# Spreading the norm's factors by two transfers, and building attention's bias rows on GpSimd

## The chip, the cores and the metric

The kernel runs on one core of one Trainium2 chip. The metric is the device time of one execution in microseconds; the median of three runs of the kernel before is 1729.15 us (1728.78 to 1729.55). One further execution was recorded by the hardware profiler, and all rows below come from it. Engines carry the profile's names: PE is the matrix engine (PEld its weight loads), DVE the vector engine, ACT the scalar engine, POOL is GpSimd, SP only issues transfers. SPq, ACTq and POOLq mark transfers that SP, ACT and POOL issue.

## The reference

A two-layer encoder trunk on 256 tokens of width 1024, in float32. Each layer is a token mixer and then an expert retrieval (PEER), with an RMS norm ahead of each of these four stages:

```python
def _rmsnorm(x, g):
    y = xf * lax.rsqrt(jnp.mean(xf * xf, axis=-1, keepdims=True) + RMS_EPS)
    return (y * g)

# layer 0: gated short convolution     layer 1: windowed attention, +-128 tokens
x = x + mixer(_rmsnorm(x, g_mixer))
x = x + _peer(_rmsnorm(x, g_ffn), w_q, subkeys, u, v)

# attention's bias: one row of 16 head values per bucket of the distance key - query
bias = rel_bias[_t5_bucket(rel)]        # rel_bias is 32 x 16
logits = where(abs(rel) <= 128, scores + bias, -1e30)
```

`_t5_bucket` gives each distance 0 to 7 a bucket of its own and then ever longer runs of distances one bucket, 16 buckets for each sign. In PEER each token finds 128 of 16384 experts by product keys; the kernel multiplies all rows of the two expert tables u and v with all tokens and weighs the unwanted ones with zero.

## The kernel before, in words

**Stages.** Convolution mixer (about the first 98 us of the profile), PEER of layer 0 (to about 868 us), attention (to about 952 us), PEER of layer 1, final norm. In each, every weight tile (128x1024, float32) is loaded by SP as `raw`, rounded to `hi` by ACT (L196), and the rest `lo` = raw - hi is formed by DVE (L197); PE then multiplies hi and lo with the two parts of the activations. `hi` has three buffers and `lo` two (in places four), so the tiles run about two ahead of PE.

**The norm's factors.** `turned_x` transposes the residual for a stage without the norm's factor; the factor, one number per token, is found meanwhile on DVE (`scale`, L419 to L428) and stands in two columns of `stat`, tokens on partitions. Later steps need it along the free dimension, the same 256 numbers on all 128 partitions: the tile `yb`. `factors` (L569) makes it: two transposes on PE of the broadcast column into a bank `pyb` of PSUM, and one copy by ACT (L574).

**Who reads `yb`.** In the convolution `mixed` (L619, L626); in PEER `normed` (L965), a background step; in attention L893 (`yq`), L895 (the two key tiles) and L896 (the first query tile). The first scores of attention (`psc`, tile 0) need L895 and L896. In PEER `yb` is later used again as `far`, which holds places and gates of the indirect additions.

**Attention's bias rows.** `load_buckets` (L744) loads, in the convolution stage, a 33x511 table of ones and zeros (which bucket, or outside the window) three times and the 32x16 values; `bias_rows` (L754) splits the values in three bfloat16 parts on DVE; `product` multiplies them by one matmul (`pbias`), DVE negates and reverses the result (L766), and POOL writes the 16x511 rows to `bias_dram`, from where they are read in PEER of layer 0.

**What sets the order.** Each engine runs its own instructions in program order as a scheduler laid them down, from the order of the code and its own estimates; `issue_after` pins one instruction behind another. POOL's queue holds, ahead of the indirect additions of a PEER stage (L706): the clearing of `table` in 1 MB pieces (L694, sixteen of them, each behind the one before), the load of the subkeys (L932), and whatever else is issued by GpSimd. Transfers issued by POOL share one queue.

Of the kernel before, what the change touches and what calls it, by code (L numbers as in the profile page):

```python
# [8 lines left out]
F32 = mybir.dt.float32  # L9
# [8 lines left out]
P = 128  # L18
# [58 lines left out]
def trunk_kernel(  # L77
# [37 lines left out]
    def transpose(*a):  # L115
        newest[:] = [PE.transpose(*a).ins]  # L116
        return newest[0]
# [15 lines left out]
    def bank(tag, name):  # L133
        if tag == "acc":
            return four_banks(False).tile([P, 512], F32, tag=tag, name=name, bufs=4)
        return ps.tile([P, 512], F32, tag=tag, name=name, bufs=2)
# [97 lines left out]
    def take(n=2):  # L234

        prefetch(n)
        return ahead.popleft()
# [76 lines left out]
    def wide_pair(b, act, between=None, last=False):  # L314

        pair = [[a.rearrange("p (k c) -> p k c", k=KC) for a in take(2 - i)] for i in range(2)]

        banks = b if isinstance(b, list) else [b[:, i] for i in range(2)]

        def one(i, k, low):  # L320
            with after_chain():
                chain[:] = [
                    matmul(banks[i][:, :T], pair[i][1][:, k], act[:, k, :T], start=False, stop=(k == KC - 1))
                    if low else matmul(banks[i], pair[i][0][:, k], act[:, k], start=(k == 0), stop=False)
                ]

        def part(i, low):
            for k in range(KC):
                one(i, k, low)

        part(0, False)
        if last:
            bg.pump()
            part(0, True)
            prefetch(1)
            for k in range(KC):
                one(1, k, False)
                one(1, k, True)
            prefetch(2)
            return bg.pump()  # L340
        if between:
            with in_turn():
                between()
        if roomy:
            prefetch(1)
            bg.pump()
        part(1, False)
        if roomy:
            prefetch(2)
        else:  # L350
            bg.pump()
        part(0, True)
        prefetch(1)
        part(1, True)
        prefetch(2)
        bg.pump()
# [209 lines left out]
            evicted[:] = [scaled]  # L566
        return xn

    def factors():  # L569

        b = bank("g", "pyb")
        for t in range(NT):
            transpose(b[:, P * t : P * t + P], stat[:, 8 + t : 9 + t].to_broadcast([P, P]), ident)
        S.copy(yb, b[:, :T])  # L574

    class Scratch:
        def __init__(self, tag, name, kb=64):
# [20 lines left out]
    def conv_mixer(sc):  # L598
        cw = sc(KC, 3)
        xn = turned_x(0, big.tile([P, KC, 2 * T], F32R, tag="xa", name="xn"))  # L600
        wait_for(nc.gpsimd.dma_start(cw, conv_w).ins, [bg.rounded])
        loaded = load_buckets(sc)
        z = big.tile([P, KC, 2 * T], F32R, tag="HB", name="z")
        ring = [(sc(2, T), sc(T + 2), sc(T)) for _ in range(2)]
        yb2 = sc(T)
        for _, ch, _ in ring:
            V.memset(ch, 0.0)

        def mixed(j, b0, b1):
            cs, ch, y = ring[j % 2]  # L610
            if j:
                sum_of_parts(cs, b0)
                V.tensor_tensor(ch[:, 1 : T + 1], cs[:, 0], cs[:, 1], ALU.mult)
                V.tensor_tensor(ch[:, 1 : T + 1], ch[:, 1 : T + 1], yb2, ALU.mult)
                gate = cs[:, 0]
                S.copy(gate, b1[:, T:])
                V.tensor_tensor(gate, b1[:, :T], gate, ALU.add)
            else:
                V.tensor_tensor(yb2, yb, yb, ALU.mult)  # L619
                V.tensor_tensor(ch[:, 1 : T + 1], b0[0][:, :T], yb2, ALU.mult)  # L620
                V.tensor_tensor(ch[:, 1 : T + 1], b0[1][:, :T], ch[:, 1 : T + 1], ALU.mult)
                gate = b1[:, :T]
            S.activation(y, ch[:, 0:T], AF.Copy, scale=cw[:, j, 0:1])
            V.scalar_tensor_tensor(y, ch[:, 1 : T + 1], cw[:, j, 1:2], y, op0=ALU.mult, op1=ALU.add)
            V.scalar_tensor_tensor(y, ch[:, 2 : T + 2], cw[:, j, 2:3], y, op0=ALU.mult, op1=ALU.add)
            V.tensor_tensor(y, y, yb, ALU.mult)  # L626
            V.tensor_tensor(y, gate, y, ALU.mult)
            S.copy(z[:, j, :T], y)
            V.tensor_tensor(z[:, j, T:], y, z[:, j, :T].bitcast(F32), ALU.subtract)

        for j in range(KC):
            roomy[:] = [True] if 0 < j < KC - 1 else []
            if j == 2:
                blank_table()
            if j == 4:
                bias_product = bias_rows(*loaded)
            if j in (2, 4, 6):
                blank_part(nc.gpsimd, bg.behind)
            b0 = two_banks("pconv") if 0 < j < KC - 1 else [bank("u", "pconv") for _ in range(2)]
            if j:  # L640
                wide_pair(b0, xn, (lambda: (factors(), mixed(*left))) if j == 1 else None)
            b1 = bank("g", "pgate")
            if j:
                wide_line(b1, xn)
            else:
                first_three([b[:, :T] for b in (*b0, b1)], xn)
            if j == 0:
                left = j, b0, b1
            else:
                mixed(j, b0, b1)  # L650
        acc = accumulators("pout")
        for k in range(KC - 2):
            rows_product(acc, take(), z[:, k, :T], z[:, k, T:], k == 0, bias_product if k == 1 else None)
            if k in (0, 3):
                blank_part(nc.gpsimd, bg.behind)
        return last_rows(acc, [(take(KC - k), z[:, k, :T], z[:, k, T:]) for k in (KC - 2, KC - 1)])
# [12 lines left out]
    def wait_for(ins, others):  # L669
        for o in others:  # L670
            tc.add_manual_dep(
                ins, o.name, mybir.DependencyInfo(mybir.DependencyClass.Sync, mybir.DependencyReason.DATA),
                reason="transfers of one table in turn",
            )
# [67 lines left out]
    bias_dram = dram.tile([HEADS, 511], F32, name="bias_dram")  # L742

    def load_buckets(sc):  # L744
        oh, ohb = sc(511)[:97], sc(256).bitcast(BF16)[:97, :511]
        rb, row = sc(HEADS)[:32], sc(511)[:HEADS]
        thirds, second = sc(HEADS // 2).bitcast(BF16), sc(HEADS // 2).bitcast(BF16)[:32]
        V.memset(thirds[96:97], NEG)
        for to, t in [(rb, relb)] + [(oh[i : i + 32], buckets[0:32]) for i in (0, 32, 64)] + [(oh[96:97], buckets[32:33])]:
            wait_for(nc.gpsimd.dma_start(to, t).ins, [bg.rounded])  # L750
        return oh, ohb, rb, thirds, second, row

    def bias_rows(oh, ohb, rb, thirds, second, row):
        with tc.issue_after(bg.behind):  # L754
            V.tensor_copy(ohb, oh)
            V.tensor_copy(thirds[0:32], rb)
            V.tensor_tensor(rb, rb, thirds[0:32], ALU.subtract)
            V.tensor_copy(second, rb)
            V.tensor_copy(thirds[32:64], rb)
            V.tensor_tensor(thirds[64:96], rb, second, ALU.subtract)  # L760

        def product():
            b = bank("g", "pbias")
            with in_turn():
                matmul(b[:HEADS, :511], thirds[:97], ohb, start=True, stop=True)
            V.tensor_scalar(row, b[:HEADS, 510::-1], -1.0, None, op0=ALU.mult)  # L766
            nc.gpsimd.dma_start(bias_dram, row)

        return product

    def load_bias(sc, part):

# [14 lines left out]
    def attention(sc, last):  # L787
# [3 lines left out]
        both = big.tile([P, 2, KC, 2 * T], F32R, tag="HB", name="xo")  # L791
        bk = [bank("u", "pk")[:, :T] for _ in range(2)]
        xn, o = turned_x(2, both[:, 0], last, bk), both[:, 1]


        ring = [(sc(2, 2, T + 1), sc(2, 2, 2, P), sc(2, 2, 2)) for i in range(3)]
# [89 lines left out]
            cols_product(b0[:, :T], take(), xn)  # L886
        pair = [bank("acc", f"pv{t}") for t in range(NT)]
        all_values(0, pair)
        with in_turn():
            factors()  # L890
        with tc.issue_after(evicted[0]):
            copied[:] = [S.activation(stat[:, 10:11], eps, AF.Exp).ins]
        V.tensor_scalar(yq, yb, -1.0 / 8.0, None, op0=ALU.mult)  # L893
# [33 lines left out]
    def peer(layer, last, meanwhile):  # L927
# [247 lines left out]
        for c in range(0, NSUB, 2):  # L1175
            q = qT[(c // 4) % 2][:, c % 4 : c % 4 + 2]
            b = two_banks("pq") if c else bq
            if c == 2:
                roomy[:] = [True]
            if c in (2, 6, 10):  # L1180
                blank_part(nc.gpsimd, bg.behind)
            if c:
                wide_pair(b, xr)
            else:
                bg.pump()
                prefetch(1)
                bg.pump()
            if c:
                sum_of_parts(q, b)
            else:  # L1190
                for i in range(2):
                    S.copy(q[:, i], b[i])
            if c == 2:
                factors()
            if c >= 4 and c % 4 == 0:
                compared(c - 4)
        bg.plan(bg.cost(), 2)
# [388 lines left out]
```

## Time and profile before

| what | value |
|---|---|
| median of three runs | 1729.15 us |
| the profiled execution | 1729.1 us, span 1727.3 us (1.8 us outside the span) |
| PE busy | 1719.7 us |
| PEld busy | 1478.1 us |
| DVE, ACT, POOL busy | 1385.1, 955.2, 960.9 us |
| clock granted to PE | 0.999 |
| instructions | 28115 |

A row of the timeline reads: start, duration, engine, line of the kernel, operation, tiles written <- tiles read, shapes, count; in brackets the idle time of that engine just before and what ended it. Matmuls overlap one another, so what one costs PE is read from the distance of starts, not from its duration. A row of waits reads: who waited <- for whom: us in total, times, longest. A row of transfers reads: tiles, issuing queue, operation, count, size of one, median us from issue to landing.

### The profile page before, as it was taken

To read this page: it belongs to the slowest core of one execution; us is meant where nothing else is said; L and a number is where in the kernel's file an instruction comes from. 1 tells how busy PE (TensorE), PEld (TensorE's weight loads), DVE (VectorE), ACT (ScalarE), POOL (GpSimd) and SP (SyncE) were. 2 spreads that over 40 slices of the span, in tenths; PEclk is the share of its full clock that TensorE was granted. 3 is DMA by queue.
4 is the path that set the end of the run, shared out by engine and by line. 5 is a ranking of instruction groups with operands and counts; after the bars stand their busy time and mean duration, and the time that the engine had idled before them with its cause. 6 is when DMAs were issued, how large, how long until landed. Compare 5 with 4: busy or idle time off the path is not lost.

```text
span 1727.3 us, 28115 instructions
## 1 busy us (share of the span) xinstructions
PE 1719.7 (100%) x9659; PEld 1478.1 (86%) x9659; DVE 1385.1 (80%) x2994; ACT 955.2 (55%) x1283; POOL 960.9 (56%) x594
## 2 busy tenths in 40 slices
PE   9999999999999999999999999999999999999998
PEld 8888888888888888888898988888888888888887
DVE  8879989888777677777686899898887867777776
ACT  6556665565555444444476666655655544444444
POOL 1002888888888888000000048888888888870000
PEclk9999999999999999999999999999999999999999
DMA  7786997777779999988765779977776899998884
GB/s 261 254 284 212 287 272 193 177 181 185 180 185 237 224 236 242 293 278 261 232 206 181 261 212 288 254 193 174 182 184 169 210 232 228 238 249 262 257 260 139
DMA packets 292383, 390.92 MB, mean 226 GB/s; under 512 B 120192, under 2 KB 209824, under 8 KB 291984
## 3 DMA queue, kind: packets, MB, share of 16 engines
q1 hardware_dynamic: 86688, 314.35, 53.5%
q0 software_dynamic: 80144, 22.83, 15.2%
q10 hardware_dynamic: 125408, 51.96, 11.5%
q8 instruction: 75, 1.23, 0.3%
q14 instruction: 68, 0.56, 0.1%
HBM read 353.08 MB, written 35.95 MB: 225 GB/s over the span
## 4 chain that ended last, share of the span: by engine, by line
PE 100%; DVE 0%; ACT 0%; issue 0%; ACTq 0%
PE ph L112 41%; PE pv L112 41%; PE pq L112 7%; PE pconv L112 3%; PE psc L112 1%; PE pwo L112 1%; PE pgate L112 1%; PE pout L112 1%; PE pg L112 1%; PE ptr L116 0%; PE ppt L116 0%; PE po L112 0%; PE pk L112 0%; PE pwarm L112 0%; PE pend L112 0%; PE pyb L116 0%
## 5 line engine op out<-in xcount | busy, mean ns | idle before, releaser
L197 DVE TENSOR_TENSOR lo<-raw,hi 128x1024 fp32r<-128x1024 f32 x592 | 717.8, 1221 | 197.6 <-ACT hi L196 136.5
L196 ACT CAST hi<-raw 128x1024 fp32r<-128x1024 f32 (+1 forms) x594 | 620.8, 1047 | 437.4 <-PE pv L112 180.5
L706 POOL DMA_INDIRECT table<-route x256 | 445.3, 1740 | 133.5 <-issue 74.7
L112 PE MATMUL pv<-hi,xn 128*128 128x512 f32 (+1 forms) x2048 | 507.8, 389 | 0.0
L112 PE MATMUL ph<-xn,hi 128*128 128x512 f32 x2048 | 491.2, 391 | 0.0
L112 PEld LDWEIGHTS pv<-hi,xn 128*128 128x128 f32 x2048 | 384.3, 188 | 79.5
L112 PEld LDWEIGHTS ph<-xn,hi 128*128 128x128 f32 x2048 | 376.3, 188 | 72.8
L706 POOL DMA_INDIRECT far_table<-yb x192 | 350.9, 1828 | 58.5 <-issue 53.4
L112 PE MATMUL pv<-lo,xn 128*128 128x512 f32 x1024 | 276.9, 390 | 0.0
L112 PEld LDWEIGHTS ph<-xn,lo 128*128 128x128 f32 x2048 | 262.6, 191 | 8.7
L112 PE MATMUL ph<-xn,lo 128*128 128x256 f32 x2048 | 269.7, 283 | 0.0
L112 PEld LDWEIGHTS pv<-lo,xn 128*128 128x128 f32 x1024 | 191.5, 188 | 39.4 <-DVE lo L197 0.3
L1321 POOL DMA_DIRECT2D far_gates<-far_table x44 | 23.8, 540 | 261.1 <-DMA gates<-table 108.5
L694 POOL DMA_DIRECT2D table<-blank x16 | 18.8, 1174 | 204.8 <-DVE lo L197 176.2
L706 POOL DMA_INDIRECT set_table<-yb x64 | 113.8, 1779 | 21.4 <-issue 21.4
L1383 ACT CAST xn<-hm 128x512 fp32r<-128x512 f32 x64 | 39.7, 623 | 68.5 <-PE pv L112 66.9
L364 ACT COPY hm<-ph 128x512 f32<-128x512 f32 x64 | 37.6, 587 | 65.4 <-PE ph L112 65.3
L1384 DVE TENSOR_TENSOR xn<-hm,xn 128x512 fp32r<-128x512 f32 x64 | 44.0, 690 | 34.8 <-ACT xn L1383 34.8
L1383 ACT CAST xn<-route 128x512 fp32r<-128x512 f32 x64 | 39.8, 622 | 50.0 <-PE pv L112 46.5
L1384 DVE TENSOR_TENSOR xn<-route,xn 128x512 fp32r<-128x512 f32 x64 | 44.1, 688 | 26.0 <-ACT xn L1383 26.0
L112 PE MATMUL pq<-xr,hi 128*128 128x512 f32 (+1 forms) x288 | 64.4, 370 | 0.0
L1361 ACT ACTIVATE hm<-hm 128x512 f32<-128x512 f32 x64 | 40.3, 630 | 35.8 <-DVE hm L365 35.6
(235 smaller groups left out, 1523.6 us busy)
## 6 DMA issues: line engine op xcount, KB each, us to landing
raw<-in_u SPq DMA_DIRECT2D x256, 512.0 KB, 4.6
raw<-in_v SPq DMA_DIRECT2D x256, 512.0 KB, 4.5
table<-blank POOLq DMA_DIRECT2D x16, 1024.0 KB
raw<-in_w_q SPq DMA_DIRECT2D x32, 512.0 KB, 3.7
gates<-table ACTq DMA_DIRECT2D x128, 128.0 KB, 3.9
raw<-in_w_in SPq DMA_DIRECT2D x23, 512.0 KB, 4.5
far_table<-blank ACTq DMA_DIRECT2D x10, 1024.0 KB, 8.1
far_gates<-far_table ACTq DMA_DIRECT2D x156, 64.0 KB, 4.3
```

The lines of the kernel that those rows point to most:

```text
L112: newest[:] = [PE.matmul(*a, **k).ins]
L196: bg.rounded = S.copy(hi[:, c], raw[:, c]).ins
L197: bg.behind = V.tensor_tensor(lo, raw, hi.bitcast(F32), ALU.subtract).ins
L364: S.copy(dst, b[:, :, T:])
L694: ins = queue.dma_start(dst, blank[:, None, :].to_broadcast([P, dst.shape[1], P])).ins
L706: nc.gpsimd.indirect_dma_start(to, bass.IndirectOffsetOnAxis(ap=places[:, c : c + 1], axis=0), gates[:, c : c + 1], None, compute_op=ALU.a ...
L1321: ins = (nc.gpsimd if i == 2 else nc.scalar).dma_start(f[:, i], part.rearrange("p (a e t) -> p a e t", a=2, e=2)).ins
L1361: S.activation(hm[:, j : j + 2], hm[:, j : j + 2], AF.Gelu)
L1383: copied[:] = [S.copy(a[:, 0], src).ins]
L1384: return V.tensor_tensor(a[:, 1], src, a[:, 0].bitcast(F32), ALU.subtract).ins
```

## The change

- `factors` no longer uses PE, PSUM and ACT. POOL issues a transfer of the two columns of `stat` to a scratch tensor in DRAM (`of_tokens`, 2x128, single elements of 4 bytes), and a second that reads the 256 numbers back to all 128 partitions of `yb`. The second waits for the landing of the first.
- It is called in the code right behind `turned_x` in the convolution, in attention, and in place c = 0 of the query loop of PEER (before: between the first two matmul groups of j = 1; between the two halves of the values; in place c = 2).
- `load_buckets` loads only the 32x16 values, turned to heads on partitions by 4-byte elements. `bias_rows` runs on POOL: one fill of the row with the outside value, and 31 copies of one value to a run of equal columns, negated. The 33x511 table is not loaded, and the splitting on DVE, the matmul and its eviction are gone.

```diff
-    def factors():
-        b = bank("g", "pyb")
-        for t in range(NT):
-            transpose(b[:, P * t : P * t + P], stat[:, 8 + t : 9 + t].to_broadcast([P, P]), ident)
-        S.copy(yb, b[:, :T])
+    def factors(n):
+        of_tokens = dram.tile([NT, P], F32, name=f"of_tokens{n}")
+        nc.gpsimd.dma_start(of_tokens.rearrange("t (p o) -> p t o", o=1), stat[:, 8 : 8 + NT, None])
+        nc.gpsimd.dma_start(yb, bass.AP(tensor=of_tokens.tensor, offset=of_tokens.offset, ap=[[0, P], [1, T]]))
@@ conv_mixer
         loaded = load_buckets(sc)
+        factors(0)
...
-            if j == 4:
-                bias_product = bias_rows(*loaded)
...
-                wide_pair(b0, xn, (lambda: (factors(), mixed(*left))) if j == 1 else None)
+                wide_pair(b0, xn, (lambda: mixed(*left)) if j == 1 else None)
...
-            rows_product(acc, take(), z[:, k, :T], z[:, k, T:], k == 0, bias_product if k == 1 else None)
+            rows_product(acc, take(), z[:, k, :T], z[:, k, T:], k == 0)
+            if k == 2:
+                bias_rows(*loaded)
@@ the bias rows
     def load_buckets(sc):
+        by_head, row = sc(32)[:HEADS], sc(511)[:HEADS]
+        turned = bass.AP(tensor=relb.tensor, offset=relb.offset, ap=[[1, HEADS], [HEADS, 32], [1, 1]])
+        wait_for(nc.gpsimd.dma_start(by_head[:, :, None], turned).ins, [bg.rounded])
+        return by_head, row
+
+    def bias_rows(by_head, row):
+        edges = [0, 1, 2, 3, 4, 5, 6, 7, 8, 12, 16, 23, 32, 46, 64, 91, 129]
+        wait_for(G.memset(row, -NEG).ins, [bg.behind])
+        for b, (near, beyond) in enumerate(zip(edges, edges[1:])):
+            runs = [(b, slice(255 + near, 255 + beyond))]
+            if b:
+                runs.append((16 + b, slice(256 - beyond, 256 - near)))
+            for at, c in runs:
+                G.tensor_scalar(
+                    row[:, c], by_head[:, at : at + 1].to_broadcast([HEADS, beyond - near]), -1.0, None, op0=ALU.mult
+                )
+        nc.gpsimd.dma_start(bias_dram, row)
@@ attention
         xn, o = turned_x(2, both[:, 0], last, bk), both[:, 1]
+        factors(2)
...
         all_values(0, pair)
-        with in_turn():
-            factors()
@@ peer
             else:
+                factors(1 + 2 * layer)
                 bg.pump()
...
-            if c == 2:
-                factors()
```

On POOL, in the convolution stage, the instructions move as follows (`mix_115` is the stage's scratch tile; rows with - are the order before, with + the order now):

```order
-L601 DMA mix_115<-in_conv_w 128x24
-L750 DMA mix_115<-in_relb 32x16
-L750 DMA mix_115<-in_buckets 32x511 x3
-L750 DMA mix_115<-in_buckets 1x7x73
+L600 DMA mix_115<-in_conv_w 128x24
+L747 DMA mix_115<-in_relb 16x32x1
+L572 DMA of_tokens_202<-stat 128x2x1
+L573 DMA yb<-of_tokens_202 128x256
 L694 DMA table<-blank 128x16x128 x4
```

The two transfers of the factors stand ahead of the first clearing of the table, and the loads of the bucket table are gone.

Further down the same queue, behind the fourth clearing of the table, the bias rows are built:

```order
+L753 MEMSET mix_115 16x511
+L759 TENSOR_SCALAR mix_115<-mix_115 16x1 x15
+L759 TENSOR_SCALAR mix_115<-mix_115 16x4 x4
+L759 TENSOR_SCALAR mix_115<-mix_115 16x7 x2
+L759 TENSOR_SCALAR mix_115<-mix_115 16x9 x2
+L759 TENSOR_SCALAR mix_115<-mix_115 16x14 x2
+L759 TENSOR_SCALAR mix_115<-mix_115 16x18 x2
+L759 TENSOR_SCALAR mix_115<-mix_115 16x27 x2
+L759 TENSOR_SCALAR mix_115<-mix_115 16x38 x2
+L762 DMA bias_dram<-mix_115 16x511
```

These 32 instructions and the write of the rows come ahead of one more clearing of the table and of the load of the subkeys.

On DVE, at the start of attention, the order before is (L893 to L896 read `yb`, L812 evicts the second query tile):

```order
L428 SCALAR_TENSOR_TENSOR stat<-stat 128x2
L197 TENSOR_TENSOR lo<-raw,hi 128x1024
L893 TENSOR_SCALAR mix_7315<-yb 128x256
L895 TENSOR_TENSOR mix_7315<-pk,yb 128x256 x2
L896 TENSOR_TENSOR mix_7315<-pq,mix_7315 128x256
L197 TENSOR_TENSOR lo<-raw,hi 128x1024 x2
L812 TENSOR_TENSOR mix_7315<-pq,mix_7315 128x256
```

and now (L885, L887, L888 and L806 are the same statements in the changed file):

```order
L428 SCALAR_TENSOR_TENSOR stat<-stat 128x2
L197 TENSOR_TENSOR lo<-raw,hi 128x1024 x2
L885 TENSOR_SCALAR mix_7331<-yb 128x256
L887 TENSOR_TENSOR mix_7331<-pk,yb 128x256 x2
L888 TENSOR_TENSOR mix_7331<-pq,mix_7331 128x256
L197 TENSOR_TENSOR lo<-raw,hi 128x1024
L806 TENSOR_TENSOR mix_7331<-pq,mix_7331 128x256
```

One weight tile's `lo` has moved ahead of the readers of `yb`; one stays behind them.

More of the change, by code (lines that the diff above doesn't have):

```diff
@@ L744, in load_buckets @@
     def load_buckets(sc):
[L745 to L763, printed above, removed]
-            with in_turn():
[L765 to L769, printed above, removed]
+        by_head, row = sc(32)[:HEADS], sc(511)[:HEADS]
[14 more added lines that the diff above has]
+        nc.gpsimd.dma_start(bias_dram, row)
     def load_bias(sc, part):
@@ L888, in attention @@
         all_values(0, pair)
-        with in_turn():
-            factors()
         with tc.issue_after(evicted[0]):
```

## The prediction

> **What bounds the kernel now.** I read the page first, then the waits of PE, then the timeline of PE and DVE around the five places that the change touches, and last the transfers.
>
> ```profile
> span 1727.3 us, 28115 instructions
> PE 1719.7 (100%) x9659; PEld 1478.1 (86%) x9659; DVE 1385.1 (80%) x2994; ACT 955.2 (55%) x1283; POOL 960.9 (56%) x594
> ...
> PE 100%; DVE 0%; ACT 0%; issue 0%; ACTq 0%
> ```
>
> ```profile
> PE pwarm L112 <- DVE blank L171: 1.1, 1, 1.1
> ```
>
> The first fence is the page: its span, its busy times, and the chain of work that ended last. PE is busy 1719.7 of 1727.3 us and the whole chain is PE. The second is the complete answer on what PE waited for: one wait, 1.1 us, at the start. So PE's own instructions, one after another, are the time. What leaves PE's queue is saved in full, wherever it stands; what leaves DVE, ACT or the transfers is worth nothing by itself; and any wait that the change puts in front of a matmul is paid in full. The sum has two sides: matmul time removed, and waits made.
>
> **What is removed from PE.** Four pairs of transposes (`pyb`) and the product `pbias`. Each is priced by the starts of the instructions around it against the same row without it.
>
> ```profile
> 17.06 2.00 PE L112 MATMUL pconv<-xn,hi 128*128 128x512 f32 x8
> 18.90 0.38 PE L116 MATMUL pyb<-ident,stat 128*128 128x128 f32 x2
> ...
> 20.95 2.08 PE L112 MATMUL pconv<-xn,lo 128*128 128x256 f32 x16
> ...
> 25.66 3.82 PE L112 MATMUL pconv<-xn,hi 128*128 128x512 f32 x16
> 29.31 2.08 PE L112 MATMUL pconv<-xn,lo 128*128 128x256 f32 x16
> ...
> 33.06 1.11 PE L112 MATMUL pgate<-xn,lo 128*128 128x256 f32 x8
> ```
>
> ```profile
> 105.80 3.82 PE L112 MATMUL pq<-xr,hi 128*128 128x512 f32 x16
> 109.46 2.07 PE L112 MATMUL pq<-xr,lo 128*128 128x256 f32 x16
> 111.37 0.38 PE L116 MATMUL pyb<-ident,stat 128*128 128x128 f32 x2
> ...
> 115.26 2.08 PE L112 MATMUL pq<-xr,lo 128*128 128x256 f32 x16
> 117.18 1.06 PE L112 MATMUL psc<-route 128*128 128x128 f32 x8
> ```
>
> ```profile
> 880.14 0.28 PE L112 MATMUL pv<-lo,xo 128*128 128x256 f32 x1
> ...
> 880.50 0.28 PE L112 MATMUL pv<-lo,xo 128*128 128x256 f32 x1
> ...
> 881.43 0.28 PE L112 MATMUL pv<-lo,xo 128*128 128x256 f32 x1
> ...
> 886.91 1.13 PE L112 MATMUL psc<-mix 64*128 64x256 f32 x8
> ```
>
> ```profile
> 76.75 1.98 PE L112 MATMUL pout<-hi,z 128*128 128x512 f32 x8
> 78.56 1.07 PE L112 MATMUL pout<-lo,z 128*128 128x512 f32 x4
> 79.47 1.07 PE L112 MATMUL pout<-hi,z 128*128 128x512 f32 x4
> ...
> 81.81 1.08 PE L112 MATMUL pout<-lo,z 128*128 128x512 f32 x4
> ```
>
> - Convolution: sixteen wide matmuls with the pair among them took 17.06 to 20.95, 3.89 us; the sixteen without it 25.66 to 29.31, 3.65. The pair costs 0.24.
> - PEER of layer 0: sixteen narrow ones, the pair and sixteen wide ones took 109.46 to 115.26, 5.80; alone they take 3.66 (105.80 to 109.46) and 1.92 (115.26 to 117.18), together 5.58. The pair costs 0.22. Layer 1 runs the same rows and is taken at the same 0.22.
> - Attention: a group of three matmuls takes 0.36 (880.14 to 880.50); the next two groups with the pair between them took 0.93 instead of 0.72. The pair costs 0.21.
> - `pbias`: eight wide matmuls take 1.81 (76.75 to 78.56); the eight with the product among them took 79.47 to 81.81, 2.34. It costs 0.53, more than two transposes.
>
> Sum: 0.24 + 2 x 0.22 + 0.21 + 0.53 = 1.42 us. That is 0.08% of the time. A difference under 0.2% (3.46 us) is about what a measurement of this kernel cannot tell from none. So from this side alone the change can only come out as "the same"; no more than 1.42 us stands on the path to be removed. The copies of `yb` on ACT, the eviction and the splitting on DVE, and the loads of the bucket table lie under a PE that does not wait, so they are priced at nothing; their cover is PE's continuous work, and they would count only where DVE or ACT is late for PE.
>
> **What is added: a trip through DRAM, in four places.** The factors are ready when the last L428 ends; `yb` is readable two transfers later. Whether that costs anything is decided on DVE, which runs in order and now waits at the first reader, and by the matmul that waits for that reader.
>
> *Attention* is the tight place.
>
> ```profile
> 879.70 0.16 DVE L428 SCALAR_TENSOR_TENSOR stat<-stat 128x2 f32<-128x2 f32 x1
> ...
> 882.41 0.30 DVE L893 TENSOR_SCALAR mix<-yb 128x256 f32<-128x256 f32 x1 [0.31 <-ACT yb L574]
> ...
> 883.28 0.42 DVE L896 TENSOR_TENSOR mix<-pq,mix 128x256 f32<-128x256 f32 x1
> 883.90 1.22 DVE L197 TENSOR_TENSOR lo<-raw,hi 128x1024 fp32r<-128x1024 f32 x1 [0.20 <-PE pv L112]
> ```
>
> The factors are ready at 879.86 (879.70 + 0.16). The first scores start at 886.91, 0.21 earlier without the pair: 886.70. Ahead of them DVE needs 1.29 us from the start of L893 to the end of L896 (882.41 to 883.70). So `yb` must be readable by 885.41, and the trip may take 885.41 - 879.86 = 5.55 us. The `lo` at 883.90, which the new order puts ahead of the readers, ends at about 884.9 and does not decide. Queued behind the waiting L885 on DVE are the `lo` of a later tile and the eviction of the second query tile; both serve matmuls behind the first scores, the `lo` those of the query tile after next, so they don't move the point.
>
> The trace of before has no such trip. What it has are these: the small transfers that ACT issues beside the stream of weights, by group and with the smallest, median and largest time from issue to landing over both groups, and the issue of a small transfer on POOL.
>
> ```profile
> DMA to landing us min/median/max: 2.4/4.9/6.8
> ```
>
> ```profile
> gates<-table ACTq DMA_DIRECT2D x128, 128.0 KB, 3.9
> ...
> gates<-set_table ACTq DMA_DIRECT2D x112, 32.0 KB, 5.2
> ```
>
> ```profile
> 82.41 0.53 POOL L767 DMA_DIRECT2D bias_dram<-mix  x1 [3.62 <-DVE mix L766]
> ```
>
> Low end: two issues alone are 1.06 us, and no trip is shorter; two of the fastest landings are 4.8 us, inside 5.55. Middle: the first transfer is 1 KB and stands alone in an empty queue, so I take the fastest landing, 2.4; the second writes 128 KB to SBUF as `gates<-table` does, whose median is 3.9 with the 512-byte pieces that its table is laid out in against 1 KB here, and I take 3.3 between fastest and median; with 0.1 for the handing over that is 5.8, which is 0.25 us too late. High end: two of the slower median are 10.4 us, 4.85 too late. Below nothing it cannot be: the scores are no earlier than PE gets to them.
>
> [...]
>
> *Convolution.*
>
> ```profile
> 17.38 0.16 DVE L428 SCALAR_TENSOR_TENSOR stat<-stat 128x2 f32<-128x2 f32 x1
> ...
> 22.15 1.22 DVE L197 TENSOR_TENSOR lo<-raw,hi 128x1024 fp32r<-128x1024 f32 x1 [0.19 <-ACT hi L196]
> ...
> 29.87 1.22 DVE L197 TENSOR_TENSOR lo<-raw,hi 128x1024 fp32r<-128x1024 f32 x1
> ```
>
> The factors are ready at 17.54 and DVE comes to the first reader (L619) at 23.37, behind four `lo`: up to 5.83 us of trip nothing is late. Beyond it every `lo` behind L619 slips. The first that PE meets is the one at 29.87, done at 31.09 and used by the `pgate` matmuls at 33.06: another 1.97 us of cover. So PE waits from a trip of 7.8 us on. At 5.8 the cost is nothing.
>
> *PEER.* In both layers the transfers stand in POOL's queue behind a 1 MB clearing of the table, so the trip is longer, but its reader is far.
>
> ```profile
> far_table<-blank ACTq DMA_DIRECT2D x10, 1024.0 KB, 8.1
> ```
>
> ```profile
> 127.79 0.68 DVE L965 TENSOR_TENSOR route<-route,yb 128x512 f32<-128x512 f32 x1
> ```
>
> A 1 MB clearing takes 8.1 us to land where its landing is recorded. The factors are ready before the transposes at 111.37; 5.8 + 8.1 later is 125.3, ahead of the first reader at 127.79. Nothing.
>
> **What is added on POOL for the bias rows.** One fill and 31 short copies; before, POOL only wrote the rows out.
>
> ```profile
> 1.30 1.50 POOL L154 IOTA iota<- 128x256 bf16 x1
> ...
> 2.86 0.69 POOL L159 IOTA place_in_set<- 32x1 f32 x4
> ...
> 87.69 1.19 POOL L694 DMA_DIRECT2D table<-blank  x1 [4.74 <-PE pout L112]
> 100.34 0.57 POOL L932 DMA_DIRECT2D route<-in_subk  x1 [11.46 <-ACT xr L484]
> ```
>
> No instruction of that kind is in the trace. Low: 32 times 0.17 us, a quarter of the 0.69, is 5.5. High: with the 511 + 257 columns at 5.9 ns each on top (1.50 us over 256 columns), 4.5 more, it is 10.0. They start when the third output tile is through, near 84 us, and end between 89.5 and 94; then come the write of the rows, the clearing and, at 100.34, the load of the subkeys, before which POOL was idle for 11.46 us. I take 7 us, and it fits: cost nothing.
>
> **Sum.** -1.42 + 0.25 + 0 + 0 + 0 = -1.17 us. The profiled execution's span goes from 1727.3 to 1726.1, its time, with 1.8 us around the span, from 1729.1 to 1727.9. The median of the runs is 1729.15, 0.05 above that execution, so the prediction is **1728.0 us**.
>
> **The rivals.**
>
> - *All hidden or nearly so* (my forecast): trips up to 6.5 us, a wait up to 0.95. Time 1727.7 to 1728.7. For it: the small size of both transfers and an empty POOL queue in attention and convolution. Against it: the margin in attention is -0.25 to 0.75 us, which is no margin. Chance 0.65.
> - *The trip takes the place of the transposes in attention*: 6.5 to 9.2 us. Two transfers at the median of `gates<-table` are 7.8, the wait is 2.25 and the time 1729.15 - 1.42 + 2.25 = 1730.0; at 9.2 convolution adds 1.4 to 3.65 and it is 1732.8. For it: the landings recorded in this trace have medians of 3.9 and 5.2, not 2.4. Against it: those run in queues with other transfers ahead. Chance 0.20. [...]
> - *Slower*: the trip is over 9.2 us, and DVE, blocked at the first reader, starves PE in both places. At 10.4 (twice the slower median) attention waits 4.85 and convolution 2.6: 1729.15 - 1.42 + 7.45 = 1735.2. It decides from 9.2 us on. Chance 0.08.
> - *POOL is slow with short copies*: at 1 us each, 32 us from 84 and 1.7 for the two issues behind them, the subkeys (1 MB) are issued at 117.7 instead of 100.34 and land, at the 8.1 us of a clearing, at 125.8; the `psc` at 117.18, which reads them, waits 8.6 us: 1729.15 - 1.42 + 8.6 = 1736.3. It decides from about 23 us of copies on, over twice my upper bound. Chance 0.03.
> - *Faster by more than 3.46 us*: PE would have to be relieved of something that no row shows it waiting for. Chance 0.02; the last 0.02 is for things not thought of, on the slow side.
>
> **How the numbers follow.** Faster 0.02; the same 0.65 + 0.20 = 0.85, with 0.01 of the slower case's edge 0.86; slower 0.12. The forecast's own range is 1727.4 to 1728.7, its ends widened below by the 0.3 that the runs of before spread around their median. The range for 8 in 10 goes up into the second case: **1727.2 to 1731.5**.
>
> **What would show it.** In the changed profile PE's instructions fall by nine matmuls, and sixteen wide matmuls in the convolution run 3.65 throughout. In the waits of PE a row `psc` <- DVE appears with 0 to 1 us; none for `pconv`, `pgate` or `pout`. The row of DVE's L885 shows a wait for a DMA, and its start less the end of L428 is the trip, 5 to 6.5 us. POOL's 32 instructions take 5 to 10 us and L924 still starts near 100 us. The prediction is wrong if `psc` waits over 3 us, if any wait for `lo` appears on PE in the convolution, or if the subkeys are issued late.

## The result and the profile after

| kernel | median us (range) | ratio to before, 95% interval |
|---|---|---|
| before | 1729.27 (1728.78 to 1729.55, 5 runs) | |
| changed | 1747.68 (1745.86 to 1749.04, 5 runs) | 1.0107 [1.0096, 1.0118] |

The change makes the kernel 18.4 us slower. The prediction was 1728.0, in a range of 1727.2 to 1731.5, so it was wrong by 19.7 us. The profiled execution of the changed kernel has a span of 1745.9 us, 18.6 over before.

First the head of the page of the changed kernel, and the shares of the chain that ended last by engine:

```profile
span 1745.9 us, 28118 instructions
...
PE 1723.5 (99%) x9650; PEld 1479.7 (85%) x9650; DVE 1382.3 (79%) x2986; ACT 949.6 (54%) x1279; POOL 1007.6 (58%) x630
...
PE 93%; DMA 3%; DVE 3%; ACT 1%; issue 1%; SPq 0%; ACTq 0%
```

PE has nine matmuls fewer (9650 for 9659), as it should. But it is busy 3.8 us longer, and the chain, all PE before, now runs 7% of its length through transfers, DVE and ACT. The complete answer on what PE waited for (total, times, longest):

```profile
PE psc L112 <- DVE mix L888: 8.1, 1, 8.1
PE pconv L112 <- ACT hi L196: 3.9, 1, 3.9
PE pgate L112 <- DVE mix L617: 1.4, 1, 1.4
PE pwarm L112 <- DVE blank L171: 1.1, 1, 1.1
PE pq L112 <- DVE route L365: 0.6, 1, 0.6
PE psc L112 <- DVE route L365: 0.5, 1, 0.5
```

Before there was one such row. The first three are 13.4 us. The first and the third are late factors; the second is a weight tile whose `hi` was late, and ACT was late because its transfer was (waits in the stretch 10 to 40 us):

```profile
ACT hi L196 <- DMA raw<-in_w_in: 12.0, 4, 9.1
DVE mix L619 <- DMA yb<-of_tokens: 10.7, 1, 10.7
POOL yb L573 <- DMA of_tokens<-stat: 8.2, 1, 8.2
```

Nothing in the change touches the weights' transfers. The windows of the same stretch show what happened to them (columns: window, its length, busy time of each engine, granted clock, share of the transfer engines, GB/s):

```profile
16.00:20.00 4.00, 4.00 (x22) 3.43 (x21) 3.73 (x9) 1.43 (x2) 0.74 (x1) 1.00 1.07 155
20.00:24.00 4.00, 4.00 (x26) 3.62 (x26) 1.91 (x2) 0.68 (x1) 0.00 (x0) 1.00 0.54 31
24.00:28.00 4.00, 2.98 (x17) 2.27 (x15) 0.00 (x0) 0.00 (x0) 1.64 (x2) 1.00 0.46 30
28.00:32.00 4.00, 1.13 (x5) 0.95 (x6) 0.00 (x0) 1.53 (x2) 0.12 (x1) 1.00 0.99 370
32.00:36.00 4.00, 4.00 (x19) 3.61 (x18) 3.34 (x7) 0.99 (x2) 0.00 (x0) 0.58 1.01 388
```

From 20 to 28 us all transfers together move 30 GB/s, a tenth of what they move right after, while the engines are far from empty (share near 0.5). Two things follow each other in this view: PE runs dry from 27.0 on (2.98 of the 4 us busy in 24:28), and then its clock is granted at 0.58 in 32:36, where 1.00 is full speed.

In attention the chain is shorter. Rows of POOL, DVE and PE of the changed kernel:

```profile
886.36 0.72 POOL L572 DMA_DIRECT2D of_tokens<-stat  x1 [41.67 <-DVE stat L428]
894.88 0.56 POOL L573 DMA_DIRECT2D yb<-of_tokens  x1 [7.80 <-DMA of_tokens<-stat]
```

```profile
885.90 0.16 DVE L428 SCALAR_TENSOR_TENSOR stat<-stat 128x2 f32<-128x2 f32 x1
...
899.78 0.29 DVE L885 TENSOR_SCALAR mix<-yb 128x256 f32<-128x256 f32 x1 [8.60 <-DMA yb<-of_tokens]
```

```profile
901.12 2.08 PE L112 MATMUL psc<-mix 64*128 64x256 f32 x8 [8.14 <-DVE mix L888]
...
907.34 1.13 PE L112 MATMUL psc<-mix 64*128 64x256 f32 x8
```

The trip takes 899.78 - 886.06 = 13.7 us: 0.3 to the issue, 0.7 issue, 7.8 until the first transfer has landed, 0.6 issue, 4.3 until `yb` is there. Then PE, which stood still for 8.14 us, runs the first scores and the query tile behind them in 6.22 us (901.12 to 907.34); the windows show why, PEclk 0.50 until 904:

```profile
896.00:900.00 4.00, 0.00 (x0) 0.00 (x0) 0.22 (x2) 0.00 (x0) 0.61 (x1) 0.50 0.96 300
900.00:904.00 4.00, 2.88 (x12) 2.06 (x13) 3.30 (x9) 0.24 (x1) 0.00 (x0) 0.50 0.59 199
904.00:908.00 4.00, 4.00 (x28) 3.82 (x29) 3.15 (x11) 2.90 (x10) 1.16 (x1) 0.78 0.35 112
```

### The profile page after: what moved, and what is told of

Its sections match the earlier page's. It is cut to its first block, busy times and chain, and to the rows that moved or that the text cites. A ratio compares the mean times of both kernels' runs of the same rounds, so it can differ in the third digit from the quotient of the medians.

```text
span 1745.9 us, 28118 instructions
## 1 busy us (share of the span) xinstructions
PE 1723.5 (99%) x9650; PEld 1479.7 (85%) x9650; DVE 1382.3 (79%) x2986; ACT 949.6 (54%) x1279; POOL 1007.6 (58%) x630
## 4 chain that ended last, share of the span: by engine, by line
PE 93%; DMA 3%; DVE 3%; ACT 1%; issue 1%; SPq 0%; ACTq 0%
PE ph L112 41%; PE pv L112 40%; PE pq L112 4%; PE pconv L112 2%; PE pwo L112 1%; PE pout L112 1%; PE pg L112 1%; PE psc L112 1%; PE pgate L112 1%; DMA of_tokens<-stat 1%; DVE lo L197 1%; DMA raw<-in_w_q 1%; DMA yb<-of_tokens 1%; PE ppt L116 0%; PE po L112 0%
## 5 line engine op out<-in xcount | busy, mean ns | idle before, releaser
L706 POOL DMA_INDIRECT far_table<-yb x192 | 370.4, 1929 | 58.6 <-issue 51.9
L706 POOL DMA_INDIRECT set_table<-yb x64 | 124.9, 1951 | 20.1 <-issue 19.2
L694 POOL DMA_DIRECT2D table<-blank x16 | 18.6, 1164 | 130.3 <-DVE lo L197 91.3
```

Source lines behind the costliest of these rows:

```text
L694: ins = queue.dma_start(dst, blank[:, None, :].to_broadcast([P, dst.shape[1], P])).ins
L706: nc.gpsimd.indirect_dma_start(to, bass.IndirectOffsetOnAxis(ap=places[:, c : c + 1], axis=0), gates[:, c : c + 1], None, compute_op=ALU.a ...
```

## The experiments

Two theories stood against each other. **The write:** 256 single elements of 4 bytes side by side in DRAM hold up every transfer of the core, and everything follows from that. **The plain trip:** a transfer to DRAM and one back take 14 us on a loaded chip, and those who wait for them pay. GpSimd's bias rows were a third suspect for a part. Every kernel below is an edit of the kernel before, except where it says otherwise; each time is set against runs of the kernel before on the same chip (1728.7 to 1728.9 us); the 18.4 us of the change belong to a chip where before took 1729.3.

### Each half of the change alone

```diff
 # bias rows only: load_buckets, bias_rows and their two calls as in the change; factors() on PE as before
 # factors only: factors(n) and its three calls as in the change; bias rows as before
```

> The kernel before with only the bias rows moved to GpSimd; the factors stay on PE. By the theory that the write of the factors does all the harm: the matmul of the bias and its wait-free place on PE are saved, 0.5 us, so 1728.7 us, within 0.2% of before, and no row of PE's waits but the one at the start. By the rival that the 32 short instructions and the new order on GpSimd cost part of the 18.4 us (a later load of the subkeys, or the turned load of the 32x16 values by 512 single elements): 1731 to 1735 us, with a wait of PE for a transfer or for GpSimd in PEER of layer 0 or in the convolution.

> The kernel before with only the factors spread by two transfers, in all four stages; the bias rows as before. By the theory that the transfers do all the harm: 18.4 + 0.5 us over before, 1748 us (1746 to 1750), with waits of PE for DVE at the first scores near 8 us and for ACT's hi in the convolution near 4 us, as in the changed kernel. By the rival that GpSimd's bias rows share in it: 1735 to 1744 us.

Bias rows only: 1728.15 us, ratio 0.9998 [0.9989, 1.0007], and PE waits for nothing but `pwarm`. Factors only: 1747.48, ratio 1.0111 [1.0095, 1.0126]. The bias rows cost nothing that can be told from noise; the transfers do all of it.

### The write alone, and the same write spread out

```diff
+    def lone(n):
+        of_tokens = dram.tile([NT, P], F32, name=f"of_tokens{n}")
+        nc.gpsimd.dma_start(of_tokens.rearrange("t (p o) -> p t o", o=1), stat[:, 8 : 8 + NT, None])
 # called where the change calls factors(n); nobody reads of_tokens
 # spread: of_tokens is [NT * P, 128], and element 0 of each row is written (512 bytes apart)
```

> The kernel before, factors on PE, and beside them the first transfer alone, in the same four places: 256 single elements of 4 bytes written into 1 KB of DRAM. Nobody reads it and nobody waits for it. By the theory that the write itself holds up every other transfer for some 8 us: weights come late in the convolution and in attention, the moved bytes fall to about 30 GB/s for two windows of 4 us behind each write, and the time is 5 to 12 us over before, 1734 to 1741. By the rival that two transfers just take 14 us and only who waits for them pays: no window falls, no wait, 1729.2 (1728.8 to 1729.8).

> As the lone write, but each of the 256 elements goes to a row of its own, 512 bytes apart, 128 KB in all. By the theory that the elements hold each other up because they fall into the same small stretch of DRAM: no window falls, 1729.2 (1728.8 to 1730). By the variant that any write of 256 single elements does it, wherever they go: as the lone write, 1734 to 1741. By the rival that only waiting for the trip costs: 1729.2.

The lone write: 1734.92 us, ratio 1.0042 [1.0027, 1.0058], 6.2 us for something that nobody reads. Spread out: 1728.68, ratio 1.0000 [0.9991, 1.0009]. Windows of 2 us of the lone write, behind its issue at 17.48:

```profile
20.00:22.00 2.00, 2.00 (x16) 1.88 (x15) 1.85 (x2) 1.34 (x3) 0.00 (x0) 1.00 0.33 35
22.00:24.00 2.00, 2.00 (x13) 1.74 (x12) 1.79 (x4) 0.00 (x0) 1.09 (x1) 1.00 0.98 35
24.00:26.00 2.00, 2.00 (x15) 1.79 (x14) 0.00 (x0) 0.00 (x0) 0.09 (x1) 1.00 0.44 33
26.00:28.00 2.00, 1.28 (x6) 0.73 (x4) 0.00 (x0) 0.00 (x0) 0.00 (x0) 1.00 0.51 170
```

What PE waited for in the same kernel:

```profile
PE pconv L112 <- ACT hi L196: 2.7, 1, 2.7
...
PE psc L112 <- DVE route L365: 0.5, 1, 0.5
```

So the plain trip is not the whole cause: there is no trip here, and time is lost. The write costs the convolution a late weight tile and the clock behind it:

```profile
30.00 3.54 PE L112 MATMUL pconv<-xn,hi 128*128 128x512 f32 x8 [2.72 <-ACT hi L196]
33.38 2.07 PE L112 MATMUL pconv<-xn,lo 128*128 128x256 f32 x16
```

The eight wide matmuls behind the wait of 2.72 us take 3.38 us to the next row, 1.5 more than eight take at full clock (1.84, 22.86 to 24.70 in the kernel before). That is 4.3 us of the 6.2; what of the rest is not the 0.5 of `psc` is not placed. In attention the bytes fall as well (66, 37, 31 and 31 GB/s in the windows of 2 us from 888 to 896), but no row of PE's waits stands there: the weights came early enough.

### The transfers in one kind of stage alone

```diff
 # convolution / attention / PEER: factors(n) by transfers there, factors_pe() (as before) in the others
```

> The kernel before with the factors spread by two transfers in attention alone; convolution and PEER keep the transposes. By the theory that the write holds up the transfers and the clock falls behind PE's wait: the first scores wait 8 us for DVE and run at half clock for 10 us, in all 10 us over before, 1739 (1737.5 to 1740.5). By the rival that attention only shows what was caused further ahead: under 5 us over before.

> The kernel before with the factors spread by two transfers in the convolution alone. By the theory: late weights (ACT's hi, near 4 us), DVE's gate (1.4 us) and the clock, 6 to 7.5 us over before, 1735 to 1736.5; the lone write without a reader already cost 6.2, so that waiting for the trip adds 1 us at most. By the rival that waiting for the trip is a cost beside the held-up weights: 9 us or more over before, over 1738.

> The kernel before with the factors spread by two transfers in both PEER stages alone. By the theory: readers are far, what is left is weights that come late: 1 to 2 us over before less 0.4 for the two pairs of transposes, 1729.5 to 1730.5. By the prediction on record, in which PEER costs nothing: 1728.3.

| where | median us | ratio | over before |
|---|---|---|---|
| attention | 1739.12 | 1.0060 [1.0043, 1.0077] | 10.4 |
| convolution | 1736.05 | 1.0040 [1.0026, 1.0054] | 7.3 |
| both PEER stages | 1731.67 | 1.0015 [1.0006, 1.0025] | 2.95 |

Together 20.7, against 18.8 for all four at once; the intervals of single runs are as wide as that difference. Attention's and convolution's shares came out as expected. The 7.3 of the convolution are 1 us more than the 6.2 of the lone write, as expected, but that write stands in four places. Set against the 4.3 us that its convolution shows, the transfers with a reader cost more there: PE waits 3.7 us for `hi`, 0.2 for the late factors, and loses 3.0 at the lower clock (mean granted clock 0.997, 0.999 before), 6.9 in all. PEER came out above its expectation. Its profile shows a wait of only 0.6 us (`psc` for DVE's `route`), but the profiled execution is the fastest of the ten (1730.16 us, 1.4 over before); where the rest of the 2.95 sits is open.

### The change, with the single elements gone

Here the changed kernel itself is edited: DVE turns the factors first, so that a partition holds 32 of them side by side, and the write is eight runs of 128 bytes in two transfers.

```diff
+    sq, sr = const.tile([P, 32], F32, name="sq"), const.tile([P, 32], F32, name="sr")
+    nc.vector.memset(sq, 0.0)
...
     def factors(n):
+        V.tensor_copy(sq[:, :NT], stat[:, 8 : 8 + NT])
+        V.transpose(out=sr, in_=sq)          # 32x32 blocks
         of_tokens = dram.tile([NT, P], F32, name=f"of_tokens{n}")
-        nc.gpsimd.dma_start(of_tokens.rearrange("t (p o) -> p t o", o=1), stat[:, 8 : 8 + NT, None])
+        for t in range(NT):
+            nc.gpsimd.dma_start(of_tokens[t].rearrange("(b j) -> b j", b=4), sr[t::32])
         nc.gpsimd.dma_start(yb, ...)         # as in the change
```

> The changed kernel with one thing else: the factors are first turned by DVE in blocks of 32x32, so that the write to DRAM is eight runs of 128 bytes in two transfers, no single elements; the read back to all partitions is unchanged. By the theory that the single elements do the harm: bytes don't fall behind the write, no late hi in the convolution; the trip is still 8 to 11 us (0.5 for DVE, two issues of 0.7, landings of 3.4 to 5), so the first scores wait 2.5 to 5 us and the time is 1730 to 1735. By the rival that two transfers through DRAM take 14 us whatever their form: first scores late by 8 us, 1739 to 1748.

1733.53 us, ratio 1.0030 [1.0020, 1.0039], 4.8 us over before. The form of the write accounts for 13.6 of the 18.4 us (18.4 - 4.8, each against its own chip). With this write, issued at 20.58, the transfers move 254 GB/s in 20:24 and 317 in 24:28, against 290 and 309 in the kernel before and 35 and 101 behind the lone write: they are not held up as there. In attention POOL and DVE now show:

```profile
883.64 1.13 POOL L577 DMA_DIRECT2D of_tokens<-sr  x2 [42.13 <-DVE sr L574]
886.43 0.57 POOL L578 DMA_DIRECT2D yb<-of_tokens  x1 [1.67 <-DMA of_tokens<-sr]
```

```profile
882.74 0.16 DVE L430 SCALAR_TENSOR_TENSOR stat<-stat 128x2 f32<-128x2 f32 x1
...
890.24 0.29 DVE L890 TENSOR_SCALAR mix<-yb 128x256 f32<-128x256 f32 x1 [2.22 <-DMA yb<-of_tokens]
```

The first landing takes 1.67 us instead of 7.80, from the same kind of memory, and the trip 890.24 - 882.90 = 7.3 us. PE's scores wait 1.77 us and then run at full clock (1.00 in 892:896):

```profile
891.58 1.13 PE L112 MATMUL psc<-mix 64*128 64x256 f32 x8 [1.77 <-DVE mix L893]
...
895.72 1.13 PE L112 MATMUL psc<-mix 64*128 64x256 f32 x8
```

From score to score it is 4.14 us here and 6.22 in the changed kernel: the idle PE's clock cost 2.1 us on top of its wait. The rest of this kernel's loss is in the convolution, where the read of `yb` now stands in POOL's queue behind a 1 MB clearing of the table (issued at 22.95, the read at 25.83, the reader on DVE at 34.18) and `pconv` waits 1.9 and 1.3 us. So 4.8 us of loss remain for the trip and its place in the queue; the three waits make 4.9, less the 1.4 removed from PE, and about 1 us is not placed.

### What sets the length of the stall

The lone write again, in other shapes. In each only the scratch tensor and the columns of `stat` differ.

```diff
 # 64 bytes apart:  of_tokens is [NT * P, 16], element 0 of each row
 # 16 bytes apart:  of_tokens is [NT * P, 4],  element 0 of each row
 # half as many:    one column of stat, [1, P]
 # sixteen:         one column of stat, 16 partitions, [1, 16]
 # pairs:           both columns as one run of 8 bytes, [P, NT]
```

> As the lone write, but the 256 elements lie 64 bytes apart, in 16 KB (512 bytes apart cost nothing, side by side 6.2 us). If what collides is a stretch of 64 bytes or less: 1728.7 (1728.3 to 1729.5) and no fall of the moved bytes. If it is a stretch of 512 bytes, in which eight elements still meet: a shorter stall, up to the 6.2 us of before, 1730 to 1735.

> As the lone write, but one column of the factors alone: 128 elements side by side in 512 bytes. If the elements go one after another (256 in some 8 us, 0.03 us each), the stall is 4 us, the two weight tiles of stock cover most of it, and the time is 1728.5 to 1731, with at most one window of 4 us at about 30 GB/s. If the stall is a fixed cost of such a write: as the lone write, 1733.5 to 1736.

> As the lone write of 256 elements, but 16 bytes apart, four in each 64 bytes, 4 KB in all. Measured so far: 64 bytes apart costs 0.2 us, side by side 6.2, and half as many side by side 5.2. If the length of the stall goes by how many elements meet in one stretch of 64 bytes (16 there: 7 to 8 us, so near 0.5 us each): four of them, about 2 us, which the weight tiles in stock cover, 1728.7 to 1729.5. If it goes by the size of the whole area, or by any two elements that touch one stretch: 5 to 6 us over before, 1734 to 1735.

> A lone write of sixteen elements only, side by side in 64 bytes of DRAM, from sixteen partitions. If the stall goes by how many elements meet in one stretch of 64 bytes: as the lone write of 256, with some 6 us at 30 GB/s, 1732 to 1735. If it goes by the number of elements in all, or by sixteen stretches being hit at once: 0 to 0.5 us over before, 1728.7 to 1729.2.

> The lone write with both factors of a partition as one run of 8 bytes, 128 runs in 1 KB, eight to each 64 bytes (which a reader would take with the tokens in another order). If the stall goes by the writes that meet in 64 bytes: half of the lone write's, about 4 us, partly covered, 1729 to 1732. If 1 KB of small writes stalls whatever their number: 1734 to 1735.

Windows behind the write, half as many first:

```profile
20.00:22.00 2.00, 2.00 (x16) 1.88 (x15) 1.58 (x2) 1.60 (x3) 0.00 (x0) 1.00 0.34 29
22.00:24.00 2.00, 2.00 (x13) 1.74 (x12) 1.93 (x4) 0.00 (x0) 0.83 (x1) 1.00 0.85 31
24.00:26.00 2.00, 2.00 (x14) 1.80 (x13) 0.12 (x1) 0.00 (x0) 0.36 (x1) 1.00 0.49 33
26.00:28.00 2.00, 1.30 (x6) 0.75 (x4) 0.00 (x0) 0.00 (x0) 0.00 (x0) 1.00 0.51 129
```

then the pairs,

```profile
20.00:22.00 2.00, 2.00 (x14) 1.80 (x13) 1.21 (x1) 1.79 (x3) 0.00 (x0) 1.00 0.71 27
22.00:24.00 2.00, 2.00 (x15) 1.82 (x15) 1.93 (x4) 0.29 (x2) 0.42 (x1) 1.00 0.57 117
24.00:26.00 2.00, 2.00 (x14) 1.84 (x13) 0.50 (x2) 0.47 (x1) 0.77 (x1) 1.00 1.03 408
```

16 bytes apart, sixteen elements, and 64 bytes apart:

```profile
20.00:22.00 2.00, 2.00 (x15) 1.84 (x14) 1.39 (x2) 1.48 (x3) 0.00 (x0) 1.00 0.65 96
22.00:24.00 2.00, 2.00 (x14) 1.78 (x13) 1.93 (x4) 0.07 (x1) 0.64 (x1) 1.00 0.98 375
```

```profile
20.00:22.00 2.00, 2.00 (x16) 1.90 (x15) 1.49 (x2) 1.70 (x3) 0.00 (x0) 1.00 0.50 154
22.00:24.00 2.00, 2.00 (x12) 1.71 (x11) 1.93 (x4) 0.39 (x1) 0.74 (x1) 1.00 1.00 410
```

```profile
20.00:22.00 2.00, 2.00 (x16) 1.88 (x15) 1.46 (x2) 1.71 (x3) 0.00 (x0) 1.00 0.93 266
22.00:24.00 2.00, 2.00 (x13) 1.74 (x13) 1.93 (x4) 0.97 (x3) 0.71 (x1) 1.00 0.93 338
```

| write | writes that meet in 64 bytes | in 256 bytes | GB/s in 20:22, 22:24, 24:26, 26:28 | us under 200 GB/s | us | ratio |
|---|---|---|---|---|---|---|
| 256 side by side | 16 | 64 | 35, 35, 33, 170 | 8.5 | 1734.92 | 1.0042 [1.0027, 1.0058] |
| 128 side by side | 16 | 64 | 29, 31, 33, 129 | 9.0 | 1733.88 | 1.0029 [1.0020, 1.0038] |
| 128 pairs of 8 bytes | 8 | 32 | 27, 117, 408, 406 | 4.5 | 1729.16 | 1.0002 [0.9992, 1.0011] |
| 256, 16 bytes apart | 4 | 16 | 96, 375, 395, 403 | 3.0 | 1728.98 | 1.0001 [0.9991, 1.0011] |
| 16 side by side | 16 | 16 | 154, 410, 246, 352 | 3.0 | 1728.93 | 1.0001 [0.9991, 1.0010] |
| 256, 64 bytes apart | 1 | 4 | 266, 338, 242, 375 | 1.0 | 1728.94 | 1.0001 [0.9992, 1.0010] |

The column "us under 200 GB/s" is the first such stretch from 18.5 us on, read in windows of half a microsecond. The kernel before, without any such write, has one of 1.0 as well (66 and 147 GB/s in 19:20), so 1 us is no stall.

Half the elements stall as long as all of them, against the expectation that they go one after another at 0.03 us each. Sixteen elements in one stretch of 64 bytes stall only briefly, against the expectation that one full stretch of 64 bytes is enough. So neither the number of writes nor the number in 64 bytes orders the rows. The number that meet in 256 bytes does: 64, 64, 32, 16, 16 and 4 writes go with 7.5, 8, 3.5, 2, 2 and 0 us above that 1 us, an estimate of 0.12 us for each write. Attention shows the same order: the transfers stay under 120 GB/s for 9, 8, 4, 2, 2 and 1 us there, in windows of 1 us, and for 1 in the kernel before. Counted in 512 bytes (128, 128, 64, 32, 16 and 8 writes) the order holds nearly as well, at some 0.06 us each; the eight writes would make 0.5 us, below what these windows show.

Both counts take it that the scratch tensor begins at such a boundary, and the runs don't decide between them. That writes to one stretch go one after another is the reading that fits; it was not shown by a run of its own. Whether a scratch row in SBUF would do better was not tried.

The column of times tells a second thing: only the two long stalls cost time. The stalls of up to 3.5 us cost none that can be measured; the weight tiles in stock cover them, and PE waits for nothing but `pwarm` in these four kernels.

### What is left of the change that does not lose

```diff
 # bias rows on GpSimd; factors by eight runs of 128 bytes in PEER only; convolution and attention on PE as before
```

> What the runs so far leave over of the change: bias rows on GpSimd, the factors by transfers in the two PEER stages alone and written as eight runs of 128 bytes (turned by DVE first), transposes on PE in the convolution and in attention. By the theory: 0.53 for the bias and 2 x 0.22 for the pairs of transposes are saved and nothing is held up, 1727.8 us, 0.05% faster, which can't be told from before. By the rival that late readers in PEER cost by themselves (PEER alone was 2.9 us slower with single elements): 1729.5 to 1731.

1728.09 us (1727.69 to 1728.41), ratio 0.9996 [0.9987, 1.0005]: 0.6 below before on its chip, so 19.0 better than the change, and not to be told from before. PE waits for nothing but `pwarm`. The prices of the removed matmuls can be read in the profile if the start is left out, where the first matmul of the convolution comes at a different time in each execution. Before it starts at 7.96 in a span of 1727.3, here at 7.93 in 1726.3:

```profile
7.96 0.71 PE L112 MATMUL pconv<-xn,hi 128*128 128x256 f32 x4
```

```profile
span 1726.3 us, 28135 instructions
...
7.93 0.71 PE L112 MATMUL pconv<-xn,hi 128*128 128x256 f32 x4
```

1719.34 and 1718.37 us from there to the end: 0.97 less, and the prediction's prices for `pbias` and two pairs are 0.53 + 0.44 = 0.97. That the two agree to the last digit is luck. The same reading of five lone writes that cost no time, with all matmuls of before, gives 1719.33 to 1719.58, and of the bias rows alone 1718.99, 0.35 less where the price is 0.53.

## Why the prediction was wrong

- **PE's chain is the time.** Right as far as the loss could be placed: each placed part is a wait of PE or its clock.
- **1.42 us removed from PE.** Right as far as it was measured: sixteen wide matmuls of the convolution now take 3.65 us, and three of the five terms showed together as 0.97 in the kernel above, to within some 0.2.
- **The trip, 5.8 us (4.8 to 10.4).** This is the step that failed. The term "I take the fastest landing, 2.4", because the first transfer "is 1 KB and stands alone in an empty queue", was measured at 7.8 to 8.2 us. Size and queue were the wrong measure of it; its form decides: with the same bytes in runs of 128 the wait for it is 1.67 us. The second term, 3.3, was 4.3. Without the single elements the trip is 7.3 us including 0.4 of DVE's turning, inside the range and inside the second case, not the first.
- **What the first transfer does to others** had no term at all. It made the convolution's weights late: the lone write in four places took 6.2 us with no reader. The bounds of the sum were bounds on the trip, so no end of the range could hold it.
- **Attention's margin, 5.55 us.** Right, and twice: 13.7 - 5.55 = 8.2 against a wait of 8.14, and 7.3 - 5.55 = 1.8 against 1.77. A margin read from the rows held; the length of the trip did not.
- **Convolution, "PE waits from a trip of 7.8 us on".** The trip was 32.63 - 17.10 = 15.5 us, which would make 7.7. The late reader made 1.4 (`pgate`), and the late weights 3.9. The loss has nearly the size that this rule gives, by another mechanism; that is luck.
- **PEER at nothing.** Wrong with single elements (1.0 to 4.3 us over before by its interval), right with runs of 128 bytes. The forecast set the length of the trip against the reader of `yb` alone; with the transfers in PEER alone the bytes fall to 100 GB/s in 118:122 of that kernel, behind the write issued at 111.2; the kernel before moves 295 there.
- **The clock.** Not in the prediction. The changed kernel runs at half clock behind both stops (0.50 in 32:35 and in 900:904). In attention that is 2.1 us. In the convolution the 24 matmuls behind the stop take 0.8 and 1.0 us longer than at full clock. The sums are then: convolution 3.9 + 1.4 + 1.8 - 0.2 = 6.9, attention 8.1 + 2.1 - 0.2 = 10.0, of the 18.6 us in the span. The two waits of 0.6 and 0.5 in PEER are about what the other removed matmuls save (0.44 + 0.53), so some 1.6 us are not placed.
- **Bias rows, 7 us (5.5 to 10.0) on POOL, at no cost.** The cost was right, the duration above its bound: 0.52 for the fill and 10.28 for 31 copies, 0.33 each on average.

```profile
87.99 0.52 POOL L753 MEMSET mix<- 16x511 f32 x1 [2.47 <-DVE lo L197]
88.60 10.28 POOL L759 TENSOR_SCALAR mix<-mix 16x1 f32<-16x1 f32 x31
```

- **The rivals.** The slower one (a trip over 9.2 us that bites in attention and convolution, 0.08) was the nearest: place and direction were right, its 1735.2 us 12.5 us short, since its trip ended at 10.4 and it had neither the held-up weights nor the clock. Of the signs named, `psc` waited over 3 us. The wait in the convolution was for `hi` and not, as named, for `lo`. The subkeys were issued late, at 106.21 for 100.34, but not because POOL was slow: its copies were done at 98.9, and the row names PE, which the convolution's loss had made late.

```profile
106.21 0.57 POOL L924 DMA_DIRECT2D route<-in_subk  x1 [5.24 <-PE pout L112]
```

## What to carry to other kernels

The form of a transfer weighed more than its size here: many small writes side by side in DRAM held up the core's other transfers for some 7 us, whether or not anyone read the result, and turning the data so that each run is 128 bytes took that away. When an edit puts a round trip where a matmul was, read the margin from the rows of the reader, and add to it the clock that PE loses behind a stop (1.5 to 3.0 us behind stops of 2.7 to 8.1 us here). A short experiment that issues the new transfer alone, with nobody waiting, tells its price to others apart from its price to its reader.

## What the runs showed that was not expected

- 128 elements of 4 bytes in 512 bytes of DRAM bring all transfers of the core down to about 30 GB/s for some 7 us, as long as 256 do; the same number as 8-byte pairs for half of that; 256 of them 64 bytes apart not at all. What orders all six writes is how many meet in 256 (or 512) bytes, not in 64.
- The stock of weight tiles covers a stall of up to 3.5 us without a measurable cost (1.0002 [0.9992, 1.0011]); at 7 us and more the kernel pays 5.2 to 6.2.
- PE's stop of 8.14 us was followed by 2.1 us of loss through the granted clock, one of only 2.72 us (the lone write) by 1.5; stops of 1.77 and 1.9 us (the kernel with runs of 128 bytes, mean granted clock 0.999) by none. The granted clock stands at 0.50 in 900:904 behind the first, at 0.50 in 30:32 behind the second, and at 1.00 from 888 to 896, around the stop of 1.77.
- A GpSimd copy of one value to 1 to 38 columns on 16 partitions takes 0.33 us on average, 0.20 to 1.31, and not in the order of the widths.
